# Attention's first value fetches and the memory keys' stores on GpSimd's DMA queue, four tiles for attention's outputs, and the last head's halves added on VectorE

## Chip, cores and metric

The kernel runs on one core of a Trainium2 chip. The metric is the device time of one execution in microseconds (us). Five engines work side by side, each through its own instructions in order: TensorE (PE in the profile; PEld is its weight load), VectorE (DVE), ScalarE (ACT), GpSimd (POOL) and SyncE (SP), which here only issues DMAs. DMAs issued on SP and on ACT go through queues marked as hardware in the profile, those issued on GpSimd through one marked as software. All move their data on the same 16 DMA engines.

## What is computed

One decoder layer on 1024 tokens of width 1024: a SwiGLU half, a mixer of two head groups side by side (stick-breaking attention, and a Mamba-2 scan called SSD), cross-attention to a memory of 256 tokens, and a second SwiGLU half, each with a norm before and after it. The change touches the stick-breaking attention and the place where the memory's keys are projected. Cut to these:

```python
def stick_breaking_attention(q, k, v):          # 16 heads of 64, blocks of 128 queries
    z = jnp.einsum('bhtd,bhsd->bhts', qb, kb) * scale
    log_1mb = jnp.where(causal, jax.nn.log_sigmoid(-z), 0.0)
    suffix = lax.cumsum(log_1mb, axis=3, reverse=True) - log_1mb
    a = jnp.exp(jnp.where(causal, jax.nn.log_sigmoid(z) + suffix, -jnp.inf))
    outs.append(jnp.einsum('bhts,bhsd->bhtd', a, vb))

def memory_cross_attention(h, mem_n, wq, wkv, wo):
    k, v = jnp.split(mem_n @ wkv, 2, axis=-1)    # 256 x 1024 each, 4 heads of 256
    ...
```

## The kernel before

Activations lie with channels on the 128 partitions and tokens along the free dimension, in two halves of 512 tokens. A float32 operand of a matmul is split into a rounded part (hi) and the rest (lo), and a product is three matmuls; the split is a cast on ScalarE (L265) and a subtraction on VectorE (L267). TensorE's instructions are held in the order in which the program is written: `_pe` (L100) chains each matmul to the one before and keeps a clock of estimated cost. Work for the other engines is put into a list with due times on that clock (`later`, run by `run_later`, L122). A scheduler places the other engines' instructions; `urgent` (L96) raises their priority.

Three stages matter here.

**The end of the SSD stage.** While the scan ends, `keys` (L1478) projects the memory's keys, eight tiles of 128 channels. Each projection goes to a PSUM tile "mm", is scaled by VectorE into a tile "sq0" (L1491), and is split into a tile "Bt" that holds two projections, hi and lo (128 x 4 x 256, 512 KB). After every second projection the tile is stored to DRAM (L1498) from SP's queue: four stores. "Bt" has a single buffer. On SP's queue lie also the loads of the weight tiles (L184).

**Values and the first pair of heads.** `value_rows` (L1898) projects attention's values for all 16 heads in two passes, takes differences of neighbouring rows, splits them into tiles "v" (4 buffers) and stores 16 of them to DRAM from GpSimd's queue (L1923, 512 KB each). Then `attention` (L1578) goes through eight pairs of heads. For pair p, `inproj` (L1633) projects queries and keys, splits them (`parts`, L1620), and copies their halves of 64 partitions into the tiles of the two heads by DMAs on SP's queue (`rows`, L1630, 128 KB each): twelve for the queries (Q and QL), eight for the keys. `fetch` (L1646) loads a head's values from DRAM into a tile "v" (512 KB), also on SP's queue; for pair 0 both fetches stand right behind the first half of the key projection, in the code behind the first four key copies. The scheduler put the first of them ahead of those.

**Attention's units.** A unit is a pair p, a head a of the two and a block c of 256 queries. `scores` (L1713) makes the products z on TensorE, a sigmoid on ScalarE (L1729) and a running product on VectorE (the scan, L1733). `transpose` (L1770) turns the result round on TensorE, splits it (L1786 on ScalarE, L1787 on VectorE) and multiplies it with the values into a PSUM tile of 128 x 256, whose first 64 partitions belong to the hi part of the values and the other 64 to the lo part. `finish` (L1741) copies it with ScalarE into one half of a tile called `both` (512 columns; the halves alternate), stores the first 64 partitions to `mix_d` in DRAM from GpSimd (L1756), and one unit later adds the other 64 partitions to the same place with an accumulating DMA from GpSimd (`added`, L1762, L1766). The very last unit, (7, 1, 3), does it otherwise: two copies of 64 partitions on ScalarE (L1749, L1750), an addition on VectorE (L1751) and one store (L1752).

Beside the units of pairs 0 to 6 TensorE runs the projections of the next pair; beside the last pair the first part of the output projection (`mix_first`) and the memory's values. Beside pair 7, `before` (L1695) also loads rows of the SSD part (tile "ev", L1700) and splits them on ScalarE and VectorE (L272, L274). After attention, `mix_out` (L1979) loads `mix_d` back in tiles "oraw" (L2001), and `resid` (L375) loads the residual stream into tiles "xl" from GpSimd (L380).

Of the kernel before, what the change touches and what calls it, by code (L numbers as in the profile page):

```python
# [10 lines left out]
F32 = mybir.dt.float32  # L11
# [7 lines left out]
P = 128  # L19
S = 1024  # L20
H = 512
# [25 lines left out]
class Kern:  # L47
# [1140 lines left out]
    def ssd(self, close):  # L1188

        nc, ap = self.nc, self.ap  # L1190
        with self.tc.tile_pool(name=self.nm("ssa"), bufs=1, reuse_waits="tile") as ep, \
# [286 lines left out]
            def keys(n0, n1):  # L1478

                mh, ml, acc, rm = env["mem"]  # L1480
                if n0 == 0:
                    self.mem_c = self.t(self.rp, [P, 2], F32, "cmem")
                    self.rms_cols([[acc]], self.mem_c)
                    yield
                for n in range(n0, n1):
                    ps = yield from self.kvproj(next(W), mh, ml)
                    if n == 0:
                        self.rms_rows(self.mem_c[:, :], rm)
                    t = self.t(self.tp, [P, H], F32, "sq0")[:, 0:MEM]
                    with self.urgent():  # L1490
                        nc.vector.tensor_tensor(out=t, in0=ps, in1=rm, op=ALU.mult)  # L1491
                    i = n % 2
                    if i == 0:
                        env["ko"] = self.t(sp, [P, 4, MEM], F32R, "Bt")
                    o = env["ko"]
                    self.split(o[:, i, :], o[:, 2 + i, :], t)
                    if i == 1:
                        nc.sync.dma_start(out=self.kv_d[n // 2][0].bitcast(F32), in_=o.bitcast(F32))  # L1498

            env = {}  # L1500
            W = self.W = self.wstream(
# [35 lines left out]
            for i, ti in enumerate((8, 10, 0, 1)):  # L1537
                ps = self.proj_now(next(W), 1)
                if i == 0:
# [6 lines left out]
                    sp = late.enter_context(self.tc.tile_pool(name=self.nm("ssb"), bufs=1, reuse_waits="tile", side="right"))  # L1546
# [24 lines left out]
            self.merge(scan, 89000, fill, 149000)  # L1571
            gates()
            self.run_all(keys(6, 8))
            self.run_later(float("inf"))
            group_norm(1)


    def attention(self):  # L1578
        nc, ap = self.nc, self.ap
        with self.pools("at", ["o", "a"], ["w"]) as (op, sp, wsp, pp):  # L1580
# [5 lines left out]
                    return self.t(pp, shape, F32, "tr", bufs=2)  # L1586
                return self.t(self.msp, shape, F32, "ms", bufs=1)

            both = self.t(self.tp, [P, H], F32, "sq0")
            turn_o = [0]  # L1590

            begin = self.t(op, [P, S], BF16, "begin")
            nc.gpsimd.memset(begin[:, 0 : S - P], 0.0)
            nc.vector.tensor_copy(begin[:, S - P : S], self.tri)
# [2 lines left out]
            for hh in range(2):  # L1597
                nc.vector.tensor_scalar(
                    out=sc[:, 4 * hh : 4 * hh + 4], in0=self.C[hh], scalar1=-0.125, scalar2=None, op0=ALU.mult
                )  # L1600
            W = self.W
            V_d = self.value_rows(sp, pp, W)
# [17 lines left out]
            def parts(src):  # L1620
                stage[0] = 1 - stage[0]
                if stage[0] == 0:
                    hi, lo = spare
                else:
                    hi, lo = (self.t(self.tp, [P, H], F32R, n) for n in ("sq1", "dg"))
                with first():
                    self.split(hi, lo, src)
                return [[x[64 * a : 64 * a + 64, :].bitcast(F32) for a in range(2)] for x in (hi, lo)]

            def rows(t, n, sl, src):  # L1630
                nc.sync.dma_start(out=t[64 * n : 64 * n + 64, sl].bitcast(F32), in_=src)  # L1631

            def inproj(p):  # L1633
                Q = [self.t(sp, [P, S], F32R, "q", bufs=3) for _ in range(2)]
                K = [self.t(sp, [P, S], F32R, "k", bufs=3) for _ in range(2)]
                V = [self.t(sp, [P, 8, P], F32R, "v", bufs=4) for _ in range(2)]
                QL = QLs[p % 2]
                heads[p] = (Q, K, V, QL)

                def evac(ps, hh):  # L1640
                    t = self.t(sp, [P, H], F32, "ev", bufs=2)
                    with first():
                        nc.vector.tensor_tensor(out=t, in0=ps, in1=self.R[hh], op=ALU.mult)
                    return t

                def fetch(a):  # L1646
                    nc.sync.dma_start(out=V[a].bitcast(F32), in_=V_d[p // 4][:, 2 * (p % 4) + a].bitcast(F32))

                def qevac(ps, sl):

                    hi, lo = parts(ps)
                    for a in range(2):
                        for d in range(2):
                            rows(Q[a], d, sl, hi[a])
                        rows(QL[a], a, sl, lo[a])

                def kevac(t, sl):

                    hi, lo = parts(t)
                    for a in range(2):  # L1660
                        rows(K[a], a, sl, hi[a])
                        rows(K[a], 1 - a, sl, lo[a])

                h0, h1 = slice(0, H), slice(H, S)
                wq = next(W)
                if p:
                    fetch(0)
                qevac((yield from self.proj(wq, 0)), h0)
                if p < 7:
                    qevac((yield from self.proj(wq, 1)), h1)  # L1670
                    wk = next(W)
                    kevac(evac((yield from self.proj(wk, 0)), 0), h0)
                    if not p:
                        fetch(0)
                    fetch(1)
                else:
                    wk = next(W)
                    kevac(evac((yield from self.proj(wk, 0)), 0), h0)
                    fetch(1)
                    last = self.proj(wq, 1)  # L1680
                    for n in range(7):
                        next(last)
                        if n % 2:
                            before(n // 2)
                        yield
                    qevac((yield from last), h1)
                last = self.proj(wk, 1)
                for n in range(6):
                    next(last)
                    if p == 7:  # L1690
                        before(3 + n)
                    yield
                kevac(evac((yield from last), 1), h1)

            def before(n):  # L1695

                if n < 8:
                    k = n
                    raw = self.t(sp, [P, H], F32, "ev", bufs=2)
                    nc.sync.dma_start(out=raw, in_=self.mix_d[8 + k][:, 0:H])  # L1700
                    self.scaled_split(self.XH[0][k], self.XL[0][k], raw, self.par("ssd_norm_g", k))
                if n == 2:
                    ready.append(next(self.Wo))
                if n == 6:
                    late.append(mix_row(0))
                if n == 8:
                    late.pop()()
# [32 lines left out]

            def finish(p, a, c, av):  # L1741
                with self.urgent():
                    n = turn_o[0] = 1 - turn_o[0]
                    o = both[:, 256 * n : 256 * n + 256]
                    out = self.mix_d[p][a * 64 : a * 64 + 64, c * 256 : (c + 1) * 256]
                    if (p, a, c) == (7, 1, 3):
                        x = self.t(sp, [P, H], F32, "ev", bufs=2)
                        x, y = x[0:64, 0:256], x[0:64, 256:512]
                        nc.scalar.copy(y, av[64:128, :])  # L1749
                        nc.scalar.copy(x, av[0:64, :])  # L1750
                        nc.vector.tensor_tensor(out=x, in0=x, in1=y, op=ALU.add)  # L1751
                        nc.gpsimd.dma_start(out=out, in_=x)  # L1752
                        added()
                        return
                    nc.scalar.copy(o, av)
                    nc.gpsimd.dma_start(out=out, in_=o[0:64, :])  # L1756
                    added()
                    lows.append((out, o[64:128, :]))
# [3 lines left out]
            def added():  # L1762

                if lows:
                    out, x = lows.pop()
                    nc.gpsimd.dma_start(out=out, in_=x, accum_op=ALU.add)  # L1766
# [3 lines left out]
            def transpose(p, a, c, A, jj):  # L1770
# [20 lines left out]
                def prod():  # L1791
                    V = heads[p][2][a]
                    if jj == 0:
                        box["av"] = self.t(self.mmp, [P, H], F32, "mm")[:, 0:256]
                    av = box["av"]
                    for j in range(2):
                        x = slice(2 - 2 * j, 4 - 2 * j)
                        for src in (ath, atl):
                            self.mm(
                                av, V[:, 2 * jj + j, :], src[:, x, :].rearrange("p a b -> p (a b)"),  # L1800
                                jj == 0 and j == 0 and src is ath, edge and j == 1 and src is atl,
                            )
                    if edge:
                        finish(p, a, c, av)
# [613 lines left out]
```

## Time and profile before

| | |
|---|---|
| median of 3 runs | 2661.96 us (2660.45 to 2662.91) |
| profiled execution | 2661.2 us |
| its span in the trace | 2659.4 us |
| granted TensorE clock, mean | 0.991 |
| memory keys' projections end, values' begin | about 1020 us |
| first product z of attention | 1149 us |
| last product with the values | 1599 us |

The profile is of one execution. A row of the timeline has the start in us from the span's start, the duration, the engine, the line of the kernel, the instruction with output and inputs by tile, and in brackets how long the engine stood idle ahead of it and what ended that. SPq marks the issue of a DMA on SP. A row of the DMA table has the output and input, the queue that issues, the count, KB each and the median time from issue to landing. A row of waits has the waiting engine, tile and line, what it waited for, the sum in us, the count and the longest. A row of windows has a stretch, its length, the busy time and instruction count of PE, PEld, DVE, ACT and POOL, then the granted clock as a share of full speed, the busy share of the DMA engines and the GB/s that they moved.

### The profile page before, as it was taken

Reading aid. Unit: us, or ns where it says so; the run is one execution under the profiler, and the core shown is the slowest. Engines: PE = TensorE matmul, PEld = TensorE weight load, DVE = VectorE, ACT = ScalarE, POOL = GpSimd, SP = SyncE. Lnnn points to the kernel's source line nnn. Section 1 sums busy time; section 2 is a strip of 40 time slices with the busy share of each in tenths; the row PEclk is TensorE's granted clock in tenths of the full one; section 3 lists DMA queues with packets and bytes.
Section 4 is the critical chain, followed back from the end, with each engine's and each line's share of the span. In section 5 each row is a group of like instructions: output and inputs, shape, how many; then the busy total and the mean of one; then the engine's idle time right before and its main releaser. Section 6 shows DMA issues by size and latency. Waiting matters only on the chain.

```text
span 2659.4 us, 36677 instructions
## 1 busy us (share of the span) xinstructions
PE 2589.6 (97%) x12786; PEld 2148.0 (81%) x12786; DVE 1939.3 (73%) x2925; ACT 1287.7 (48%) x2229; POOL 661.7 (25%) x819
## 2 busy tenths in 40 slices
PE   9899999999999999979999999999999999999999
PEld 7688888778777887868888797888878788888887
DVE  6778897779689783356777777767566888776777
ACT  7434444555356562345565645346554433333553
POOL 2555553110100000412223211101011555552000
PEclk9899999999999999989999999999999999999999
DMA  6458888875655223775554646637648453236654
GB/s 224 163 190 281 281 277 289 276 246 169 228 187 178 88 80 120 223 202 127 147 147 120 182 136 229 215 123 254 213 161 296 157 171 123 93 101 220 192 170 151
DMA packets 211290, 493.94 MB, mean 186 GB/s; under 512 B 27617, under 2 KB 36129, under 8 KB 211105
## 3 DMA queue, kind: packets, MB, share of 16 engines
q1 hardware_dynamic: 156272, 360.56, 41.2%
q0 software_dynamic: 31504, 88.56, 11.1%
q10 hardware_dynamic: 23328, 42.48, 4.3%
q8 instruction: 100, 1.64, 0.3%
q14 instruction: 86, 0.70, 0.1%
HBM read 327.46 MB, written 138.87 MB: 175 GB/s over the span
## 4 chain that ended last, share of the span: by engine, by line
PE 82%; DVE 7%; issue 4%; DMA 4%; ACT 2%; POOL 1%; SPq 0%; DVEq 0%; ACTq 0%; POOLq 0%
PE mm L138 42%; PE dn L138 31%; PE z L138 2%; DVE nb L1733 2%; PE ms L138 1%; PE tr L141 1%; PE y L138 1%; PE ms L141 1%; PE seg L138 1%; PE tr L138 1%; DVE atl L1787 1%; PE st L138 0%; DVE hl L267 0%; SPq L1631 0%; DMA oraw<-mix 0%
## 5 line engine op out<-in xcount | busy, mean ns | idle before, releaser
L138 PE MATMUL mm<-xh,whi 128*128 128x512 f32 x1192 | 470.0, 404 | 3.6 <-ACT xh L265 2.7
L138 PE MATMUL mm<-xl,whi 128*128 128x512 f32 (+1 forms) x1124 | 438.6, 390 | 4.7 <-DVE xl L267 4.1
L138 PE MATMUL mm<-xh,wlo 128*128 128x512 f32 x1144 | 439.0, 392 | 0.0
L138 PEld LDWEIGHTS mm<-xh,whi 128*128 128x128 f32 x1192 | 225.3, 189 | 45.5 <-ACT xh L265 3.9
L138 PEld LDWEIGHTS mm<-xh,wlo 128*128 128x128 f32 x1144 | 215.2, 188 | 46.6 <-DVE wlo L267 0.4
L138 PEld LDWEIGHTS mm<-xl,whi 128*128 128x128 f32 x1124 | 212.6, 189 | 39.1 <-DVE xl L267 6.2
L1733 DVE TENSOR_TENSOR_SCAN nb<-nb,begin 128x128 f32<-128x128 f32 (+7 forms) x128 | 169.9, 1349 | 57.0 <-ACT nb L1729 56.8
L267 DVE TENSOR_TENSOR wlo<-wraw,whi 128x1024 fp32r<-128x1024 f32 x78 | 95.3, 1222 | 89.1 <-ACT whi L265 88.7
L265 ACT CAST whi<-wraw 128x1024 fp32r<-128x1024 f32 (+1 forms) x95 | 92.4, 972 | 115.7 <-PE mm L138 60.3
L1729 ACT ACTIVATE nb<-z,scale 128x128 f32<-128x128 f32 (+2 forms) x192 | 105.4, 582 | 68.4 <-PE z L138 68.0
L657 ACT ACTIVATE ft<-ft 128x512 f32<-128x512 f32 x88 | 55.5, 632 | 103.9 <-DVE ft L656 101.9
L138 PE MATMUL dn<-xh,wlo 128*128 128x512 f32 x296 | 101.2, 390 | 0.0
L740 POOL TENSOR_TENSOR wc<-wraw,raw 128x512 f32<-128x512 f32 x56 | 80.4, 1435 | 65.3 <-DVE whi L267 17.8
L740 POOL TENSOR_TENSOR wc<-raw,wraw 128x512 f32<-128x512 f32 x55 | 81.1, 1474 | 51.7 <-DVE wlo L267 21.8
L1786 ACT ACTIVATE ath<-tr,small 128x512 fp32r<-128x512 f32 (+1 forms) x106 | 68.3, 646 | 50.9 <-PE tr L141 49.1
L1787 DVE SCALAR_TENSOR_TENSOR atl<-tr,ath 128x512 fp32r<-128x512 f32 (+1 forms) x106 | 65.7, 625 | 36.0 <-ACT ath L1786 35.5
L825 POOL TENSOR_TENSOR ft<-ft,e 128x512 f32<-128x512 f32 x37 | 59.7, 1613 | 121.3 <-DVE e L824 45.1
L138 PE MATMUL z<-k,q 128*128 128x128 f32 (+2 forms) x192 | 68.0, 358 | 21.4 <-DMA k<-dg 12.7
L138 PE MATMUL mm<-ath,v 128*128 128x256 f32 x320 | 88.6, 299 | 0.0
L1766 POOL DMA_DIRECT2D mix<-sq x63 | 51.9, 823 | 138.6 <-DMA mix<-sq 123.8
L138 PE MATMUL dn<-xh,blk 128*128 128x512 f32 x264 | 85.2, 389 | 0.0
L138 PE MATMUL mm<-atl,v 128*128 128x256 f32 x320 | 83.2, 282 | 0.5 <-DVE atl L1787 0.5
(600 smaller groups left out, 6976.5 us busy)
## 6 DMA issues: line engine op xcount, KB each, us to landing
whi<-dwhi SPq DMA_DIRECT2D x74, 512.0 KB, 3.6
wlo<-dwlo SPq DMA_DIRECT2D x74, 512.0 KB, 4.8
wraw<-in_w_gu SPq DMA_DIRECT2D x43, 512.0 KB, 3.9
raw<-in_w_gu SPq DMA_DIRECT2D x37, 512.0 KB, 4.1
wraw<-xs SPq DMA_DIRECT2D x56, 256.0 KB, 3.0
xs<-ft ACTq DMA_DIRECT2D x54, 256.0 KB, 3.3
raw<-xs SPq DMA_DIRECT2D x54, 256.0 KB, 3.4
act<-ft ACTq DMA_DIRECT2D x52, 256.0 KB, 2.3
```

The source lines that it names most:

```text
L138: self._pe(self.nc.tensor.matmul(out, lhsT, rhs, start=start, stop=stop, skip_group_check=self.more), cost)
L141: self._pe(self.nc.tensor.transpose(out, src, self.ident if ident is None else ident), 109.0)
L265: self.kp(self.nc.scalar.copy(hi, src))
L267: self.nc.vector.tensor_tensor(out=lo, in0=src, in1=hi.bitcast(F32), op=ALU.subtract)
L657: nc.scalar.activation(t, t, AF.Silu)
L740: nc.gpsimd.tensor_tensor(out=t, in0=a, in1=b, op=op)
L825: nc.gpsimd.tensor_tensor(out=t1, in0=t1, in1=e, op=ALU.mult)
L1729: nc.scalar.activation(nb[:, s0:s1], z[:, 0:n], AF.Sigmoid, scale=sc[:, i : i + 1])
L1733: nc.vector.tensor_tensor_scan(out=nb[:, 0:Wd][:, ::-1], data0=nb[:, 0:Wd][:, ::-1], data1=begin[:, S - Wd : S][:, ::-1], initial=0.0, op0 ...
L1766: nc.gpsimd.dma_start(out=out, in_=x, accum_op=ALU.add)
L1786: nc.scalar.activation(hi, x, AF.Identity, bias=self.minus)
L1787: nc.vector.scalar_tensor_tensor(out=lo, in0=x, scalar=-1.0, in1=hi.bitcast(F32), op0=ALU.add, op1=ALU.subtract)
```

## The change

Four edits. The store of the memory's keys is issued on GpSimd's queue in place of SP's. Both value fetches of pair 0 are issued on GpSimd's queue; those of the other pairs stay on SP's. The tile `both` and its alternating halves are gone: `finish` takes a tile "o" of its own from attention's pool `wsp`, which held nothing in this stage, with four buffers. And all four units of the last head, (7, 1, 0) to (7, 1, 3), are now copied in two halves, added on VectorE and stored once; before, only the last was, in a tile "ev".

```diff
                     if i == 1:
-                        nc.sync.dma_start(out=self.kv_d[n // 2][0].bitcast(F32), in_=o.bitcast(F32))
+                        nc.gpsimd.dma_start(out=self.kv_d[n // 2][0].bitcast(F32), in_=o.bitcast(F32))
...
-            both = self.t(self.tp, [P, H], F32, "sq0")
-            turn_o = [0]
-
...
                 def fetch(a):
-                    nc.sync.dma_start(out=V[a].bitcast(F32), in_=V_d[p // 4][:, 2 * (p % 4) + a].bitcast(F32))
+                    (nc.sync if p else nc.gpsimd).dma_start(out=V[a].bitcast(F32), in_=V_d[p // 4][:, 2 * (p % 4) + a].bitcast(F32))
...
             def finish(p, a, c, av):
                 with self.urgent():
-                    n = turn_o[0] = 1 - turn_o[0]
-                    o = both[:, 256 * n : 256 * n + 256]
+                    o = self.t(wsp, [P, H], F32, "o", bufs=4)
                     out = self.mix_d[p][a * 64 : a * 64 + 64, c * 256 : (c + 1) * 256]
-                    if (p, a, c) == (7, 1, 3):
-                        x = self.t(sp, [P, H], F32, "ev", bufs=2)
-                        x, y = x[0:64, 0:256], x[0:64, 256:512]
+                    if (p, a) == (7, 1):
+                        x, y = o[0:64, 0:256], o[0:64, 256:512]
                         nc.scalar.copy(y, av[64:128, :])
                         nc.scalar.copy(x, av[0:64, :])
                         nc.vector.tensor_tensor(out=x, in0=x, in1=y, op=ALU.add)
                         nc.gpsimd.dma_start(out=out, in_=x)
                         added()
                         return
+                    o = o[:, 0:256]
                     nc.scalar.copy(o, av)
                     nc.gpsimd.dma_start(out=out, in_=o[0:64, :])
                     added()
```

## The prediction

> **What bounds the kernel now.** I read the page's first line of busy times, then the windows of ten microseconds around the edited lines, then the timeline of TensorE with the wait ahead of each matmul.
>
> ```profile
> span 2659.4 us, 36677 instructions
> PE 2589.6 (97%) x12786; PEld 2148.0 (81%) x12786; DVE 1939.3 (73%) x2925; ACT 1287.7 (48%) x2229; POOL 661.7 (25%) x819
> 1020.00:1030.00 10.00, 5.72 (x30) 4.40 (x30) 3.50 (x8) 3.41 (x6) 0.18 (x1) 0.98 0.48 157
> 1140.00:1150.00 10.00, 0.52 (x3) 0.55 (x3) 0.69 (x1) 1.90 (x2) 0.00 (x0) 0.50 0.92 246
> 1028.78 0.50 PE L138 MATMUL mm<-whi,xh 128*128 128x512 f32 x1 [4.28 <-DVE sq L1491]
> 1149.48 0.44 PE L138 MATMUL z<-k,q 128*128 128x128 f32 x1 [12.68 <-DMA k<-dg]
> 1492.86 0.44 PE L138 MATMUL z<-k,q 128*128 128x384 f32 x1 [2.28 <-ACT nb L1729]
> ```
>
> TensorE is busy for 97% of the span, so the change can only take from the rest, 69.8 us, of which little lies at its lines. A window row gives the stretch, its length, the busy time of PE, PEld, DVE, ACT and POOL, the granted clock, the share of the DMA engines and GB/s. PE stands still three times near the edits: 4.28 us behind the memory's keys, 12.68 us until the first pair's keys arrive, 2.28 us in the last pair. In the long stop the clock falls to 0.50 (second window row); I take it that a shorter stop moves the slow stretch behind it and does not shorten it, and leave it out of the sum.
>
> **The keys' store (L1498).** Four stores of 512 KB leave SP's queue for GpSimd's.
>
> ```profile
> 1022.03 0.33 SPq L184 DMA_DIRECT2D wraw<-in_w_v  x1
> 1022.45 0.38 SPq L1498 DMA_DIRECT2D kv<-Bt  x1
> 1027.40 0.41 ACT L265 CAST Bt<-sq 128x256 fp32r<-128x256 f32 x1 [4.78 <-DMA kv<-Bt]
> DMA to landing us min/median/max: 2.6/3.8/5.0
> out<-F POOLq DMA_DIRECT2D x8, 256.0 KB, 2.5
> out<-F SPq DMA_DIRECT2D x8, 256.0 KB, 2.0
> v<-v POOLq DMA_DIRECT2D x16, 512.0 KB, 7.0
> ```
>
> The tile Bt has one buffer, so ScalarE's next cast waits for the third store to land, 4.9 us after its issue; then VectorE frees the bank that PE wants. Behind the store on SP stands no load that was due: its next one waits for a buffer. So what counts is the landing, and that store shares the engines with a weight load issued 0.42 us ahead of it. GpSimd is free: it is busy for 0.18 us of the window from 1020 to 1030. The same 256 KB output takes 2.5 us by GpSimd and 2.0 by SP, so I take **+0.5 us**. The ends: 2.6 us, the shortest of the four, is a gain of 2.3; 7.0 us, the 512 KB stores on GpSimd's queue, a loss of 2.1. The other three stores have nothing on the path behind them. What is queued behind a waiting store on GpSimd are the attention's first memsets, and PE reads nothing of theirs before 1149.
>
> **The first pair's values (L1647).** Two fetches of 512 KB leave SP's queue, where they stand between row copies.
>
> ```profile
> 1140.81 1.08 SPq L1631 DMA_DIRECT2D wraw<-xl  x1
> 1142.19 0.47 SPq L1647 DMA_DIRECT2D v<-v  x1
> 1143.44 0.54 SPq L1631 DMA_DIRECT2D k<-dg  x1
> 1134.14 0.84 POOL L1923 DMA_DIRECT2D v<-v  x1 [1.51 <-DVE ev L1643]
> v<-v POOLq DMA_DIRECT2D x3, 512.0 KB, 9.1
> k<-dg SPq DMA_DIRECT2D x2, 128.0 KB, 5.7
> k<-dg SPq DMA_DIRECT2D x14, 128.0 KB, 2.9
> 1141.00:1142.00 1.00, 0.00 (x0) 0.00 (x0) 0.00 (x0) 0.00 (x0) 0.00 (x0) 0.50 0.77 203
> 1142.00:1143.00 1.00, 0.00 (x0) 0.00 (x0) 0.00 (x0) 0.00 (x0) 0.00 (x0) 0.50 0.59 178
> 1143.00:1144.00 1.00, 0.00 (x0) 0.00 (x0) 0.00 (x0) 0.00 (x0) 0.00 (x0) 0.50 0.88 193
> 1166.58 0.36 PE L138 MATMUL mm<-ath,v 128*128 128x256 f32 x1
> ```
>
> SP is done with the query rows at 1141.89 us (1140.81 + 1.08). The fetch and its waits end at 1142.67, and only then the first pair's key rows go out: 0.78 us goes with certainty. What is ahead of that, the query rows, issued slowly while the DMA engines are full, the change doesn't touch. The row PE waits for is the key copy issued at 1143.44, which lands 5.7 us later (1149.1), where the same copy takes 2.9 over the whole run.
>
> On GpSimd the fetch comes after the last value store (1134.14), whose bytes are out some 9 us later, at 1143.2. So it cannot be ahead of the keys by much; it fills what the engines leave idle in the three rows from 1141 to 1144, 0.23 + 0.41 + 0.12 = 0.76 us. I take both: **-1.5 us**. The ends: a clear landing of 2.9 us gives -0.78 - 2.8 = -3.6; with both fetches (1.05 MB) served ahead of the keys at 203 GB/s, +5.2 - 0.78 = +4.4. I stay near the middle, at the idle time that the rows show. The values themselves are first read at 1166.58, more than 20 us after; and GpSimd's next store is of the product that reads them, so nothing queued behind the fetches is due before.
>
> The Trainium skill, "DMA: Bandwidth & Descriptors", section "Queues, rings and completion order", says that each DMA engine goes round the queues that have work, a packet at a time. It speaks against the edit: a fetch on another queue is still beside the keys. By it the first head's 256 KB would meet as much of the fetch instead of 512 KB ahead of it, which at 193 GB/s saves 1.3 us and with the issue 2.1: the sum would be 0.6 us lower. No row here shows two queues' shares, so this stays outside the sum.
>
> **Four tiles for the outputs (L1743 to L1755).** ScalarE's copy no longer waits until both stores of its half have landed.
>
> ```profile
> ACT sq L1755 <- DMA mix<-sq: 14.1, 8, 3.2
> 1248.57 0.37 ACT L1755 COPY sq<-mm 128x256 f32<-128x256 f32 x1 [1.60 <-DMA mix<-sq]
> 1244.17 4.20 DVE L1733 TENSOR_TENSOR_SCAN nb<-nb,begin 128x896 f32<-128x896 f32 x2
> 1249.01 0.66 PE L141 MATMUL tr<-ident,nb 128*128 128x128 f32 x4 [0.34 <-DVE atl L1787]
> 1490.87 0.37 ACT L1755 COPY sq<-mm 128x256 f32<-128x256 f32 x1 [1.69 <-DMA mix<-sq]
> 1482.11 2.90 SPq L1700 DMA_DIRECT2D ev<-mix  x2
> 1488.46 0.72 ACT L272 ACTIVATE xh<-ev,params 128x512 fp32r<-128x512 f32 x1 [1.45 <-DMA ev<-mix]
> 1491.89 0.75 DVE L274 SCALAR_TENSOR_TENSOR xl<-ev,params,xh 128x512 fp32r<-128x512 f32 x1 [1.93 <-ACT xh L272]
> 1500.00:1510.00 10.00, 7.51 (x46) 6.00 (x46) 9.65 (x11) 6.64 (x14) 3.21 (x6) 1.00 0.72 190
> 1508.81 0.55 PE L141 MATMUL tr<-ident,nb 128*128 128x128 f32 x3 [2.32 <-DVE nb L1733]
> ```
>
> Eight waits, 14.1 us, read like the prize and are not. Seven are in pairs 0 to 6, as at 1248.57: there VectorE's scans run from 1244.2 to 1248.4 and PE waits 0.34 us for VectorE; ScalarE had time. Only the eighth (1.69 us at 1490.87) has PE behind it: the sigmoids queued after the copy end PE's 2.28 us, and VectorE then works with hardly a gap (9.65 of the ten microseconds from 1500) until PE takes its scan at 1508.81, so what is won there is won for good. But the next cast on ScalarE needs a load issued by 1485.0; if that one takes as long as the one before (1482.11 to 1488.46), it lands at 1491 and nothing is won. Ends 0 and -1.69, and +1.0 if the new order of ScalarE's queue puts copies ahead of work that PE waits for and doubles the 0.34 us of the row at 1249.01 in three pairs. I take half: **-0.9 us**. GpSimd's own waits between a store and its accumulation stay. The four tiles take memory of a pool that was empty in this stage; I find no load that waits for it and cost that at nothing, up to the +1.0 just named.
>
> **The last head by VectorE.** Units (7,1,0) to (7,1,2) do what only (7,1,3) did.
>
> ```profile
> 1599.12 0.39 PE L138 MATMUL mm<-atl,v 128*128 128x256 f32 x1 [0.52 <-DVE atl L1787]
> 1599.78 0.37 ACT L1749 COPY ev<-mm 64x256 f32<-64x256 f32 x1 [1.76 <-PE mm L138]
> 1600.56 0.42 DVE L1751 TENSOR_TENSOR ev<-ev 64x256 f32<-64x256 f32 x1 [1.50 <-ACT ev L1750]
> 1600.62 0.82 POOL L1766 DMA_DIRECT2D mix<-sq  x1 [2.08 <-DMA mix<-sq]
> 1606.24 4.62 POOL L380 DMA_DIRECT2D xl<-h  x7 [3.62 <-PE mm L138]
> ```
>
> Each adds a copy of 0.37 us on ScalarE and an addition of 0.42 on VectorE, and takes an accumulating DMA of 0.82 from GpSimd. The first two lie under a full PE. The third lands where PE waits for VectorE (1599.12): its addition ahead of that split costs **+0.4 us**; ends -0.3 (the accumulations no longer use the DMA engines) and +0.8 (copy and addition). The end of the stage gains nothing: GpSimd's next loads wait for PE at 1606, not for the accumulation at 1600.62.
>
> **Sum.** 0.5 - 1.5 - 0.9 + 0.4 = -1.5 us. The profiled execution took 2661.2 us (span 2659.4), 0.76 below the median shown, 2661.96; so 2659.7 there, and **2660.5** as a median.
>
> **Rivals.** About 0.2%, 5.3 us, is what a measurement of this kernel can tell from no change.
>
> *All three stops open.* The keys land clear (-3.6), the copy's whole wait goes (-1.69), the store of memory's keys takes the median of 3.8 instead of 4.9 (-1.1), the last head costs 0.4: -6.0, **2656.0**. For it: the DMA engines are at 0.59 in the very microsecond where the keys are issued. Against it: 9.1 us for the stores that still run then.
>
> *GpSimd's transfers stand in the way (slower).* Its fetches are served ahead of the keys (+4.4) and its store of memory's keys takes the 7.0 us of GpSimd's stores (+2.1), with -0.9 and +0.4: +6.0, **2668.0**. It decides from the point where the key copies land over 6.5 us (5.7 + 0.78) after their issue. For it: the engines are at 0.92 from 1140 to 1150. Against it: the fetch queues behind GpSimd's own last stores.
>
> *The change doesn't do what it says.* The copy's wait goes, the ev load ends last in its place, and the keys gain only SP's 0.78: 0.5 - 0.78 + 0.4 = +0.1, **2662.1**.
>
> **How the numbers follow.** The forecast gets 0.45, the third rival 0.14, open stops 0.25, GpSimd in the way 0.16. So faster by over 0.2% has 0.25, within 0.2% 0.59, slower 0.16. The range reaches from a little past the first rival, 2655.5, to 2666.5, short of the second; about 2 in 10 is left out.
>
> **What would show it.** Right: key rows issued at about 1142.0 with no fetch between them, PE's first z at 1147 to 1148.5; no wait of the copy L1755 for a DMA; PE back at about 1029.3 after the keys. Wrong: key copies that land later than 5.7 us after issue; another order of ScalarE's queue with new PE waits in pairs 0 to 6; a wait of over a microsecond near 1599.

## The result, and the profile after

The changed kernel takes 2666.97 us (median of 20 runs, 2658.38 to 2670.93), the kernel before 2662.47 in the same comparison (20 runs, 2657.38 to 2669.70). The ratio is 1.0015, interval 1.0007 to 1.0023: slower by 2 to 6 us, where 1.5 us of gain had been forecast. The profiled execution took 2669.86 us, its span is 2667.9.

First the timeline of PE of the changed kernel, with the waits at the places of the edits:

```profile
span 2667.9 us, 36670 instructions
1016.47 0.36 PE L138 MATMUL mm<-xs,whi 128*128 128x256 f32 x1 [0.75 <-DVE sq L1491]
1020.49 0.36 PE L138 MATMUL mm<-xs,whi 128*128 128x256 f32 x1 [0.92 <-DVE sq L1491]
1026.26 0.77 PE L138 MATMUL mm<-whi,xh 128*128 128x512 f32 x1 [0.98 <-DVE sq L1491]
1032.34 0.50 PE L138 MATMUL mm<-whi,xh 128*128 128x512 f32 x1 [1.69 <-DVE sq L1491]
1155.57 0.44 PE L138 MATMUL z<-k,q 128*128 128x128 f32 x1 [16.86 <-DMA k<-dg]
1498.09 0.44 PE L138 MATMUL z<-k,q 128*128 128x384 f32 x1 [2.93 <-ACT nb L1726]
1606.14 0.39 PE L138 MATMUL mm<-atl,v 128*128 128x256 f32 x1 [0.49 <-DVE atl L1783]
1631.01 1.84 PE L138 MATMUL ms<-small,asum 128*128 128x1 f32 x8 [3.01 <-DVE asum L1993]
```

At the memory's keys four short stops, 4.34 us together, stand where one of 4.28 and one of 1.26 were. The stop before the first pair's scores grew from 12.68 to 16.86 us. The stop in the last pair is 2.93 in place of 2.28. At 1606 (1599 before) nothing changed, and a stop of 3.01 us for the sum of squares is new.

Two executions differ also where nothing was edited: the second kernel falls 3.5 us behind near 540 us, in the first feed-forward half, and other executions below move there by 0 to 5 us. So I read profiles stage by stage: for each instruction that both have, the later start in the other execution, and per stretch the median of that; such stage figures are worked out from the traces, and no row below shows them. The stretch of the memory's keys gained 1.28 us, the first pair lost 2.81, pairs 0 to 6 gained 0.05, the last pair lost 1.95, the start of the mixing projection lost 1.34: +4.8 together, close to the +4 of the timed runs.

What SyncE issued around the first pair's key rows, and then what GpSimd did, in the timeline of the changed kernel:

```profile
1143.79 1.57 SPq L1628 DMA_DIRECT2D wraw<-xl  x1
1145.46 0.53 SPq L181 DMA_DIRECT2D wlo<-dwlo  x1
1146.23 0.46 SPq L1628 DMA_DIRECT2D k<-sq  x1
1146.78 0.72 SPq L1628 DMA_DIRECT2D k<-dg  x1
1136.69 0.64 POOL L1644 DMA_DIRECT2D v<-v  x1
1139.89 0.55 POOL L1644 DMA_DIRECT2D v<-v  x1 [2.56 <-DMA v<-v]
```

The fetch is gone from SyncE, and **a weight load of 512 KB stands in its place** (1145.46): the scheduler filled the hole. In the kernel before, that load (wlo) came behind all key rows, and only its other half (whi) ahead of the last query rows:

```profile
1130.64 1.22 SPq L181 DMA_DIRECT2D whi<-dwhi  x1
1149.62 0.54 SPq L181 DMA_DIRECT2D wlo<-dwlo  x1
```

GpSimd issued the fetches at 1136.69 and 1139.89, while SyncE's query rows (the last, into a tile that the program calls wraw, ends at 1143.79 + 1.57 = 1145.36) were still going out. Nothing was won in order, and the bytes came earlier.

The DMA view of the ten microseconds 1132 to 1142, first of the kernel before, then of the changed one (q0 is GpSimd's queue, q1 is SyncE's; packets, MB, share of the 16 engines), and of the changed one from 1145.5 to 1150.5 (KB each, us from issue to landing):

```profile
q0 software_dynamic: 431, 1.55, 51.8%
q1 hardware_dynamic: 624, 1.33, 44.9%
```

```profile
q0 software_dynamic: 479, 1.75, 62.0%
q1 hardware_dynamic: 500, 1.12, 38.9%
...
wlo<-dwlo SPq DMA_DIRECT2D x1, 512.0 KB, 9.1
...
k<-dg SPq DMA_DIRECT2D x2, 128.0 KB, 7.9
```

GpSimd's share rose by ten points and SyncE's fell by six. (The changed kernel is some 2.5 us later in this stage; its window from 1134.5 to 1144.5 shows 64.9 and 35.2%.) The key copies land 7.9 us after their issue, the median of two, where they took 5.7. The delay is there already in the query row ahead of them on SyncE's queue, issued at 1140.81 before and at 1143.79 after:

```profile
wraw<-xl SPq DMA_DIRECT2D x1, 128.0 KB, 4.1
```

```profile
wraw<-xl SPq DMA_DIRECT2D x1, 128.0 KB, 9.1
```

Last, the granted clock behind the stop (windows of two microseconds; the clock is the third number from the end), before and after:

```profile
1154.00:1156.00 2.00, 2.00 (x7) 1.41 (x7) 0.96 (x1) 0.49 (x1) 0.00 (x0) 0.54 1.02 385
1156.00:1158.00 2.00, 2.00 (x12) 1.73 (x11) 1.25 (x2) 1.74 (x3) 0.00 (x0) 1.00 0.80 317
```

```profile
1157.00:1159.00 2.00, 2.00 (x7) 1.71 (x6) 0.51 (x2) 0.47 (x1) 0.00 (x0) 0.51 1.04 250
1159.00:1161.00 2.00, 2.00 (x12) 1.70 (x12) 1.05 (x2) 0.81 (x2) 0.00 (x0) 1.00 1.00 257
```

Before, PE ran at half speed from 1149.48 to about 1155.9, 6.4 us; after, from 1155.57 to about 1159.0, 3.4 us. Half of the difference, 1.5 us, comes back: 4.18 - 1.5 = 2.7, which is the stage's loss of 2.81.

### The profile page after: what moved, and what is told of

The parts are those of the page before. It is cut to its first block, busy times and chain, and to the rows that moved or that the text cites. A ratio compares the mean times of both kernels' runs of the same rounds, so it can differ in the third digit from the quotient of the medians.

```text
span 2667.9 us, 36670 instructions
## 1 busy us (share of the span) xinstructions
PE 2592.1 (97%) x12786; PEld 2152.1 (81%) x12786; DVE 1941.8 (73%) x2928; ACT 1289.4 (48%) x2232; POOL 662.8 (25%) x822
## 4 chain that ended last, share of the span: by engine, by line
PE 67%; issue 16%; DVE 7%; DMA 6%; ACT 2%; POOL 1%; SPq 1%; DVEq 0%; ACTq 0%; POOLq 0%
PE mm L138 32%; PE dn L138 28%; PE z L138 2%; DVE nb L1730 1%; PE tr L141 1%; PE ms L138 1%; PE ms L141 1%; PE tr L138 1%; DMA wraw<-in_w_dn 1%; DMA raw<-xs 1%; DMA raw<-in_w_dn 1%; DVE atl L1783 1%; DVE hl L267 1%; DMA oraw<-mix 1%; DMA wraw<-xs 0%
## 5 line engine op out<-in xcount | busy, mean ns | idle before, releaser
L265 ACT CAST wlo<-wc 128x512 fp32r<-128x512 f32 x79 | 49.1, 621 | 70.8 <-PE dn L138 28.1
```

What stands on the lines that cost most here:

```text
L265: self.kp(self.nc.scalar.copy(hi, src))
```

## The experiments

**My theory:** the fetch edit loses, and the stores' edit gains a part of it back. **Rivals:** within the loss, that the weight load's place does it and not the fetches; and for the whole, that the difference is scatter tied to no edit. First each edit alone.

**The stores alone.**

```diff
-                        nc.sync.dma_start(out=self.kv_d[n // 2][0].bitcast(F32), in_=o.bitcast(F32))
+                        nc.gpsimd.dma_start(out=self.kv_d[n // 2][0].bitcast(F32), in_=o.bitcast(F32))
```

> The kernel before with only the four stores of the memory's keys on GpSimd's queue. By the stages of the two profiles (theory: the parts act in their own stages): a gain of about 1.3 us, since the value rows begin 1.3 us earlier there, with ScalarE's casts of Bt in another order than before. By the recorded step: a loss of 0.5 us. By the rival (the difference of the two profiles is scatter that belongs to no line): within 1 us of before. Either way PE's stop of 4.28 us behind VectorE at the third store should have become several short ones of 0.7 to 1.7 us.

Measured 2661.67 against 2663.87, ratio 0.9987 (0.9978 to 0.9995): a gain. The third store and the cast that waits for it, in the timeline of GpSimd and ScalarE, and the two stops of PE:

```profile
1028.20 0.53 POOL L1498 DMA_DIRECT2D kv<-Bt  x1 [7.21 <-DVE Bt L267]
1031.31 0.41 ACT L265 CAST Bt<-sq 128x256 fp32r<-128x256 f32 x1 [2.92 <-DMA kv<-Bt]
1026.64 0.65 PE L138 MATMUL mm<-whi,xh 128*128 128x512 f32 x1 [1.11 <-DVE sq L1491]
1032.68 0.50 PE L138 MATMUL mm<-whi,xh 128*128 128x512 f32 x1 [1.46 <-DVE sq L1491]
```

From issue to the cast are 3.1 us; before they were 4.95. GpSimd's queue as such is not the faster one: over the four stores the landing took 2.6, 3.8 and 5.0 us (shortest, median, longest) on SyncE, and here

```profile
DMA to landing us min/median/max: 2.9/3.7/4.4
```

The third store no longer follows a weight load by 0.42 us: those nearest to it were issued some 5 us ahead and 1.5 us behind. That this is what made it shorter fits, but no run shows it alone. And ScalarE's order changed: between the casts of Bt now stand casts of weights that stood elsewhere. The stage gained 1.97 us.

**The fetches alone.**

```diff
-                    nc.sync.dma_start(out=V[a].bitcast(F32), ...)
+                    (nc.sync if p else nc.gpsimd).dma_start(out=V[a].bitcast(F32), ...)
```

> The kernel before with only the first pair's two fetches of values on GpSimd's queue. By the stages of the two profiles: a loss of about 2.8 us; PE's stop before the first product of queries and keys grows from 12.7 to about 16.9 us, the key copies land 8 us or more after their issue, and a weight load of 512 KB stands on SP ahead of the key rows. By the recorded step: a gain of 1.5 us, stop about 11 us, key copies at most 5.7 us. By the rival (scatter): a stop within 1 us of 12.7.

Measured 2669.25, ratio 1.0019 (1.0010 to 1.0027): **this edit alone is the loss**. The stop of PE, and the key copies in the DMA view:

```profile
1156.34 0.45 PE L138 MATMUL z<-k,q 128*128 128x128 f32 x1 [17.47 <-DMA k<-dg]
```

```profile
k<-dg SPq DMA_DIRECT2D x2, 128.0 KB, 8.3
```

PE, VectorE and ScalarE have the same order of instructions as before; only SyncE's and GpSimd's queues differ. The first pair's stretch lost 3.8 us.

**Four tiles alone.**

```diff
-                    n = turn_o[0] = 1 - turn_o[0]
-                    o = both[:, 256 * n : 256 * n + 256]
+                    o = self.t(wsp, [P, H], F32, "o", bufs=4)[:, 0:256]
```

> The kernel before with only four tiles for attention's outputs. PE, VectorE and SyncE have the same order of instructions as before. By the stages of the two profiles: nothing in pairs 0 to 6, and in the last pair the copy's wait of 1.69 us for its store is gone while the next load of the state-space rows ends last, so between 0 and +2 us. By the recorded step: a gain of 0.9 us. By the rival (scatter): nothing, and the 2 us lost in the last pair of the changed kernel do not come again.

Measured 2664.84, ratio 0.9999 (0.9987 to 1.0010): nothing that can be told from zero. In the last pair, ScalarE's load wait and PE's next two stops on ScalarE:

```profile
1487.50 0.72 ACT L272 ACTIVATE xh<-ev,params 128x512 fp32r<-128x512 f32 x1 [0.65 <-DMA ev<-mix]
1491.69 0.44 PE L138 MATMUL z<-k,q 128*128 128x384 f32 x1 [0.45 <-ACT nb L1727]
1496.00 0.44 PE L138 MATMUL z<-k,q 128*128 128x384 f32 x1 [1.14 <-ACT nb L1727]
```

The copy no longer waits, and the load of the SSD rows came early enough here: the stage gained 0.97. (Two runs without the four tiles, the stores alone above and the held fetches below, gained 0.74 and 1.08 there, so this gain is not shown to be the tiles'.) In the changed kernel the same load was waited for longer, and the gain did not come:

```profile
1495.49 0.72 ACT L272 ACTIVATE xh<-ev,params 128x512 fp32r<-128x512 f32 x1 [3.90 <-DMA ev<-mix]
```

The edit is not what lost 1.95 us there: the run with the fetches alone lost 1.82 in the same stretch, without the four tiles. Over all 14 profiles of this study PE's stop goes with the load. Where it was waited for at most 1.45 us, the stop is 0.41 to 0.45 with four tiles (three profiles) and 1.26 to 2.28 without (three); where it was waited for 2.25 us and more, 2.93 and 3.17 with four tiles and 1.87 to 4.83 without (six). But what the tiles win there comes back in part at the next stop on ScalarE: 1.14 above, 1.19 and 2.75 in the two other early profiles with four tiles, and 0.49 to 1.19 in the three without. Over the whole stretch the early profiles gained 0.46 to 1.11 us with four tiles and 0 to 1.08 without. A gain of the stage by the tiles is not shown.

**The last head alone.**

```diff
-                    if (p, a, c) == (7, 1, 3):
-                        x = self.t(sp, [P, H], F32, "ev", bufs=2)
+                    if (p, a) == (7, 1):
+                        x = self.t(wsp, [P, H], F32, "o", bufs=4)
```

> The kernel before with only the last head's halves added by VectorE (three more units, through tiles of the same empty pool). By the stages of the two profiles: 0.3 us where PE waits for VectorE's split near 1599, and up to 1 us more at the start of the mixing projection, where VectorE, ScalarE and SyncE now have another order (casts of weights behind those of rows, a wait of PE for the sum of squares of about 3 us in place of several short ones): +0.3 to +1.3 us. By the recorded step: a loss of 0.4 us, at the end of attention alone. By the rival (scatter): within 0.5 us.

Measured 2664.99, ratio 1.0001 (0.9992 to 1.0010). Its stage lost 1.37 us, at two places of PE's timeline:

```profile
1599.92 0.38 PE L138 MATMUL mm<-atl,v 128*128 128x256 f32 x1 [0.48 <-DVE atl L1787]
1626.01 1.02 PE L138 MATMUL ms<-small,asum 128*128 128x1 f32 x8 [3.04 <-DVE asum L1997]
```

The wait for VectorE's split is what it was (0.52 before). The stop of 3.04 us is at the sum of squares, in the order that the scheduler made new behind it; it stands in each of the three profiles with this edit (3.01, 3.04, 3.35) and is 0 to 1.12 in the eleven without. What it costs is less sure, for the held fetches below lost 1.5 us in the same stretch without this edit. In the whole time the edit can't be told from zero.

Singly the four give -0.13, +0.19, -0.01 and +0.01%: +0.06, against +0.15 (0.07 to 0.23) together; each has about 0.09 of uncertainty, so the sum does not contradict.

**Which of the two costs the keys: the fetches or the weight load?** Four kernels make a square: the fetches early on GpSimd or behind the keys, the loads ahead of the key rows on SyncE or behind them. The fetches alone, above, are the corner with both ahead. In the next, manual dependencies hold the weight loads and the second pair's first fetch behind the last key row. Two loads of 512 KB move by that: wlo, which took the fetch's place, and whi, which stood ahead of the last query rows in the kernel before too. (In the diff `loads` are these two, `x` is the fetch.)

```diff
+                self.row = nc.sync.dma_start(out=t[64 * n : 64 * n + 64, sl].bitcast(F32), in_=src).ins
...
+                if p == 1:
+                    for y in self.loads + [x]:
+                        self._after(y, self.row)
```

> The fetches of the first pair's values on GpSimd, as in the change, but on SyncE's queue nothing stands any more between the first pair's row copies: the weight load that had taken the fetch's place, its other half and the second pair's first fetch are ordered behind the last key row. If the loss of the fetch edit comes from GpSimd's fetches, which share the DMA engines with the row copies: PE's stop stays at 15 to 17 us and the whole at +3 to +5 us against before. If it comes from the weight load that went ahead of the key rows on SyncE (rival): the stop falls to 9 to 12 us and the whole to -0.8 to -3.6 us. By the recorded step, which did not see the weight load: -1.5 us, which is the rival's side.

```profile
1151.55 0.45 PE L138 MATMUL z<-k,q 128*128 128x128 f32 x1 [13.61 <-DMA k<-sq]
```

Measured 2665.66 against 2663.93, ratio 1.0009 (1.0001 to 1.0018). Neither theory held alone: the stop lies between the two ranges. In the other corner the same order is kept and the fetches too go behind the keys, on SyncE:

```diff
+                if not p:
+                    for a in range(2):
+                        x = fetch(a).ins
+                        self._after(x, self.row)
+                        self.row = x
```

> The fetches stay on SyncE but behind the first pair's last key row, and the same weight loads and fetch of the second pair behind them; GpSimd's queue as before. If what is issued ahead of the key rows, on whichever queue, is what they wait for: PE's stop falls to 9 to 11.5 us (512 KB less ahead of the first head's keys at about 193 GB/s is up to 2.7 us, and 0.78 us of issue), the whole -1.2 to -3.5 us. If the stop is set by the query rows and the value stores alone (rival): the stop falls by the 0.78 us of issue at most. The values are then first late if the product that reads them waits, at about 1166.

```profile
1142.14 0.44 PE L138 MATMUL z<-k,q 128*128 128x128 f32 x1 [7.43 <-DMA k<-sq]
```

```profile
k<-dg SPq DMA_DIRECT2D x2, 128.0 KB, 2.4
```

Measured 2660.82, ratio 0.9990 (0.9980 to 1.0000). The stop is lower than I had thought possible, the stage gains 6.25 us, the whole only some 3; in this profile the last pair gives 2.6 back. The last corner leaves the loads ahead and holds the fetches on GpSimd by a copy of one column:

```diff
+                        nc.gpsimd.tensor_copy(V[a][:, 0, 0:1], K[a][:, H - 1 : H])
+                        fetch(a)
```

> The fetches on GpSimd, each behind a copy of one column of the first half of the key tile into the value tile, so that GpSimd cannot issue them before the first half of the key rows has landed; the weight load stays ahead of the key rows on SyncE as in the change. If GpSimd's fetches are the cause by sharing the engines: the stop comes back to 11 to 13 us and the whole to -1 to +0.5 us. If the weight load's place is the cause (rival): the stop stays at 15 to 17 us and the whole at +3 to +5 us. The copy adds two GpSimd instructions that nothing waits for before the values are read.

```profile
1151.27 0.45 PE L138 MATMUL z<-k,q 128*128 128x128 f32 x1 [10.14 <-DMA k<-dg]
```

Measured 2663.26, ratio 1.0007 (0.9997 to 1.0016); the stop is below the 11 to 13 us expected. Stop of PE, landing of the last query row, and landing of the key copies (median of two) behind it, in us:

```
                                  loads ahead of key rows   row copies uninterrupted
fetches early, on GpSimd              17.47   9.2   8.3         13.61   8.1   6.7
fetches behind the keys               10.14   2.6   3.8          7.43   3.3   2.4
(kernel before: 12.68, 4.1, 5.7: the first fetch ahead of the keys, on SyncE)
```

Both cost, and nearly add: the fetches 7.3 and 6.2 us of stop, the loads 3.9 and 2.7. The stretch of the first pair tells the same: against the kernel before +3.81 and +0.25 us in the first line, -3.17 and -6.25 in the second. So in the profiles the larger part is the fetches, and the weight loads add about half of that again; each theory named one. The middle number shows where the fetches act: with them early the last query row lands over 8 us after its issue, whether loads stand behind it or not, and with them late after about 3.

The square moves whi and wlo together and does not part them. But the held fetches answer for wlo in the fetch's place: there it stands as in the change, and the stop is 10.14 where it was 12.68. So the load took back what the hole was to win, and the loss against the kernel before comes with the early fetches.

In whole times the square runs 1.0019, 1.0009, 1.0007, 0.9990 in the same order, less cleanly. By them the fetches cost 0.12 and 0.19%, the loads 0.10 and 0.17, each to about 0.13, which does not tell the larger from the smaller. And the run with held fetches should be faster than before by its first-pair stretch, and its interval does not show it. That stays open.

**The good parts together.** The stores' edit, and the fetches behind the keys. "Late fetches" means here and below the whole order of the run above with 7.43 us, with both loads and the second pair's first fetch behind the key rows too; the diffs show only a part of it.

```diff
-                        nc.sync.dma_start(out=self.kv_d[n // 2][0].bitcast(F32), in_=o.bitcast(F32))
+                        nc.gpsimd.dma_start(out=self.kv_d[n // 2][0].bitcast(F32), in_=o.bitcast(F32))
...
+                        x = fetch(a).ins
+                        self._after(x, self.row)
```

> The four stores of the memory's keys on GpSimd (as in the change) together with the late fetches of the run before the last on SyncE. If both act in their own stages and the keys do wait for what is issued ahead of them: -2.2 - 2.4 = -4.6 us, between -3 and -6.5. If only the stores gain (rival): -2 to -3.5 us.

```profile
1146.38 0.45 PE L138 MATMUL z<-k,q 128*128 128x128 f32 x1 [8.05 <-DMA k<-dg]
```

Measured 2656.79, ratio 0.9979 (0.9968 to 0.9990). The 5.6 us lie where both act, though the interval, 2.7 to 8.5, reaches into the range for the stores alone. The profile shows both: the keys' stretch gains 1.2 us and the first pair's 5.1.

**What the stores' edit gains by.** The stores stay on SyncE, and a free tile of another tag takes every second pair of projections:

```diff
-                        env["ko"] = self.t(sp, [P, 4, MEM], F32R, "Bt")
+                        env["ko"] = (
+                            self.t(ep, [P, S], F32R, "Ct", bufs=2).rearrange("p (a b) -> p a b", a=4) if n in (2, 6)
+                            else self.t(sp, [P, 4, MEM], F32R, "Bt")
+                        )
```

> The kernel before, stores of the memory's keys on SyncE as they were, but every second pair of key tiles goes into a free tile of another tag, so that ScalarE's cast no longer waits for the store ahead of it to land. If the landing of a store is what the stores' edit gains by (it became shorter on the other queue, 3.1 us for 4.9, and the casts of weights went ahead): PE's stop of 4.28 us falls to under 1.5 us and the whole to -2 to -5 us, at least as much as the stores on GpSimd gave. If the stores' edit gained by freeing SyncE's queue (rival): the stop is still there, in part behind SyncE, and the whole within 1 us of before.

Measured 2656.26 against 2664.06, ratio 0.9972 (0.9962 to 0.9982): some 7.5 us, more than the 2 to 5 expected. A window of the stretch where PE stood for 4.28 us of ten:

```profile
1025.00:1035.00 10.00, 10.00 (x47) 8.36 (x48) 2.86 (x6) 2.14 (x4) 1.32 (x3) 1.00 0.62 214
```

PE is busy throughout and the clock stays at 1.00. The stage gains 7.9 us: stops of 5.5 and most of the rest from the clock, which before fell to half for some 3 us behind the long stop. So it is the landing of the store that costs, and the shorter landing of the stores' edit is the lesser cure: 2.0 us in the stage for 7.9. The stop went while the stores stayed on SyncE, so freeing that queue is not needed for it.

**And the other two parts on top.** First four tiles with the stores' edit and the late fetches (the diffs are those shown):

```diff
+                    o = self.t(wsp, [P, H], F32, "o", bufs=4)[:, 0:256]
```

> The stores of the memory's keys on GpSimd, the first pair's fetches on SyncE behind the key rows, and four tiles for attention's outputs. Against the same without the four tiles (-0.21%): by the recorded step 0.9 us faster, so about -0.24%; by the reading that the load of the state-space rows ends last in the place of the copy's wait (rival): no difference that can be measured, -0.15 to -0.25%.

Measured 2655.66, ratio 0.9968 (0.9957 to 0.9979): 0.11% better than without the four tiles, with intervals that overlap. Then the changed kernel whole, with the late fetches:

```diff
-                    (nc.sync if p else nc.gpsimd).dma_start(out=V[a].bitcast(F32), ...)
+                    return nc.sync.dma_start(out=V[a].bitcast(F32), ...)
...
+                        self._after(x, self.row)
```

> The changed kernel with one part put another way: the first pair's fetches on SyncE behind the key rows, and no load between the row copies. If the fetches are what made the change slower: -3 to -6.5 us against before, where the change was +4. If the change's loss lies elsewhere or in the parts together (rival): 0 or slower. Against the run without the last head's edit: +0.3 to +1.3 us by the stage read from the profiles, 0.4 by the recorded step.

```profile
1141.74 0.45 PE L138 MATMUL z<-k,q 128*128 128x128 f32 x1 [7.28 <-DMA k<-dg]
```

Measured 2657.72, ratio 0.9972 (0.9963 to 0.9982), where the change has 1.0015: **the order around the first key rows is worth 0.43% of the kernel**, some 11 us, and turns its loss into a gain. In the two profiles 8.2 us of it are in the first pair's stretch. It is not the place of the two fetches alone, since both loads moved as well; for the fetches alone the square has 0.12 and 0.19%. The last head's edit costs nothing that these runs can tell (0.9972 against 0.9968).

Last, what the experiments point to: the second tile in place of the stores' edit, the late fetches, and four tiles.

```diff
+                            self.t(ep, [P, S], F32R, "Ct", bufs=2).rearrange("p (a b) -> p a b", a=4) if n in (2, 6)
...
+                        self._after(x, self.row)
...
+                    o = self.t(wsp, [P, H], F32, "o", bufs=4)[:, 0:256]
```

> The second tile for the memory's keys (stores on SyncE as in the kernel before), the first pair's fetches on SyncE behind the key rows, and four tiles for attention's outputs; no edit of the last head. If the three act in their own stages: -7.0 us for the second tile (-0.28%) less what the late fetch adds to it (-0.10% alone, -0.21 + 0.13 = -0.08% on top of the stores' edit) and four tiles (-0.0 to -0.1%): -9 to -13 us against before, -0.35 to -0.5%. If the second tile and the late fetch gain at each other's cost, because the weights' loads that either sets free meet in the same microseconds (rival): -7 to -8.5 us, no better than the single parts.

```profile
1137.16 0.45 PE L138 MATMUL z<-k,q 128*128 128x128 f32 x1 [7.58 <-DMA k<-sq]
```

Measured 2650.10 against 2665.02, ratio 0.9942 (0.9928 to 0.9955): faster than the kernel before by some 15 us. That is more than the 9 to 13 expected of the parts, with an interval (12 to 19 us) that reaches into it. In the profile the keys' stage gains 7.9 us and the first pair 6.3, as in the runs of each alone.

## Why the prediction was wrong, step by step

**The fetches: forecast -1.5, measured +0.19%, about +5 us alone. This is the step that failed.** Three sentences carry it. "0.78 us goes with certainty": the queue did not close up over the hole, since the scheduler that places SyncE's instructions put a weight load of the same 512 KB there. I had moved one instruction in a fixed order, though the order is worked out anew from the whole program. "So it cannot be ahead of the keys by much; it fills what the engines leave idle": I had let the fetch begin where the bytes of the last store end, at 1143.2, but GpSimd issued it right behind the issue of that store, at 1136.69. And of the query rows I wrote that "the change doesn't touch" them: they were still to go through the same 16 engines, the last one landed 9.1 us after its issue for 4.1, and the key rows stand behind it. The view that shows two queues' shares (51.8 and 44.9% above) was there for the kernel before, and I left it out of the sum. By the square the early fetches cost 6 to 7 us of stop and the two loads 3 to 4, of which wlo's part is not known. The kernel before stands between the corners: the first fetch ahead of the keys, its issue and whi made 5.2 us together there (12.68 to 7.43).

**The sign was named rightly by a rival.** Key copies that land more than 6.5 us after issue were to decide for the slower rival; they took 7.9. Its price for the fetches, +4.4, is close to the 4.18 by which the stop grew, in part by luck, since it knew nothing of the weight load. Its total, 2668.0, is close to 2666.97, by luck too: it also charged 2.1 us for the stores, which gained.

**The stores: forecast +0.5, measured -0.13% (-0.22 to -0.05).** The place was right, since the landing of the third store holds the cast and the second tile removed the stop. The size failed, with its sign: I took the comparison of 256 KB outputs elsewhere in the kernel (2.5 to 2.0) as the nearest row, and on GpSimd the store took 3.1 us for 4.95. The change of queue is not what those rows measure: the median of the four stores hardly moved (3.8 to 3.7), and the third no longer shared the engines with a load issued just ahead of it.

**Four tiles: forecast -0.9, measured -0.01% alone and -0.11% on top of two other edits, both within the noise.** The copy's wait went, as forecast, but the stage's gain is not shown: with an early load the next stop grows, with a late one the load takes the copy's place. That the load of SSD rows would take the copy's place as the last to end was right for the changed kernel, where it was waited for 3.90 us.

**The last head: forecast +0.4.** Not there: the wait at 1599 stayed (0.52, then 0.49). A stop of 3 us came at the sum of squares, where the scheduler reordered; the stage lost 1.3 to 2.2 us in the three profiles that have the edit, but 1.5 in one without, and the whole time does not show it.

**The clock.** That a shorter stop moves the slow stretch behind it "and does not shorten it" was off by 1.5 us here, in the direction that hid a part of the loss: 6.4 us at half speed before, 3.4 after.

## What to carry to other kernels

Where a scheduler fills the queues, taking a transfer off a queue does not bring the next one forward: look up what it will pull into the hole, or order the urgent transfers by a dependency. A transfer that nothing needs for 20 us belongs behind the urgent ones, and another queue is not behind: here that order, for two fetches and two weight loads, was worth some 11 us. And where a single buffer waits for its store, a second buffer can be worth more than a faster store: here 7.9 us of the stage against 2.0.

## What was unexpected of the hardware

**The queue with larger packets got more of the engines' time.** In the ten microseconds shown of the changed kernel GpSimd's queue moved 479 packets and SyncE's 500, nearly turn by turn, but of 3.7 and 2.2 KB (1.75 MB by 479, 1.12 by 500): 62% against 39% of the engines. The same rule as in the prediction (the Trainium skill, "DMA: Bandwidth & Descriptors", section "Queues, rings and completion order": an engine takes a packet of each queue in turn) agrees with that row, if both queues had work throughout, which the row does not tell. Other windows do not have equal turns: the kernel before has 431 and 624 packets, and with the early fetches and nothing between the row copies the counts were 547 and 369:

```profile
q0 software_dynamic: 547, 2.00, 74.6%
q1 hardware_dynamic: 369, 0.60, 24.1%
```

**A stop costs more than its length, and not always the same.** Behind stops of 16.86, 12.68 and 7.43 us PE ran 3.4, 6.4 and about 4 us at half clock. Around the first two the clock stood at half for the same 17.1 us (from 1141.9 to 1159.0 after, from 1138.8 to 1155.9 before); the longer stop left less of that to PE. Behind the stop of 2.3 us that both kernels have near the end of attention's scores, the clock stayed in one profile and fell in the other; before, then after:

```profile
1510.00:1512.00 2.00, 2.00 (x17) 1.87 (x16) 1.76 (x4) 1.73 (x5) 0.83 (x1) 1.00 0.08 7
```

```profile
1513.88 0.88 PE L141 MATMUL tr<-ident,nb 128*128 128x128 f32 x3 [2.33 <-DVE nb L1730]
...
1515.00:1517.00 2.00, 2.00 (x6) 1.61 (x5) 0.69 (x1) 2.00 (x5) 0.83 (x1) 0.50 0.02 3
```

The second execution lost 1.5 us by it, three quarters of what the last pair seemed to lose. The Trainium skill, "TensorE: Matmul & The Clock Gate", section "What's actually happening", has a free-running window of about 3.4 us after which the clock is halved or restored, so that the same stop can cost differently by where it falls. The 17.1 us agree with five such windows, and the half clock behind the stop of 2.33 us, from 1513.9 to 1517.4, with one; the 3.4 and 6.4 us are only what the stop left of the last windows. The stop of 2.33 us that was enough once is shorter than the idle window that the same section of the Trainium skill asks for.
